# Splitting a tile's softmax probabilities one tile later, with exp written to PSUM

## The chip, the cores and the metric

The kernel runs on one core of a Trainium2 chip. The metric is device time in microseconds (us) for one execution, from the median of several runs. Engines are named as the profile names them: PE is TensorE's matmul, PEld its weight load, DVE is VectorE, ACT is ScalarE, POOL is GpSimd, and SP is SyncE, which issues every DMA of this kernel. Each engine works through its own instructions strictly in order and waits for the others by semaphores.

## The reference, cut to what matters

The reference is a two-layer decoder trunk on 1024 tokens of width 1024, in float32. Layer 0 is a pooling branch plus an attention into 256 memory tokens. Layer 1, where the change lies, has a "forgetting" attention with 16 heads of width 64. For each block of 128 queries it computes this:

```python
logits = jnp.einsum('bqhd,bkhd->bhqk', qi, k, preferred_element_type=jnp.float32) * scale
logits = logits + (ci[..., :, None] - cum_k[:, :, None, :])
qpos = s0 + jnp.arange(Q_BLOCK)
mask = kpos[None, :] <= qpos[:, None]
logits = jnp.where(mask[None, None], logits, -jnp.inf)
p = jax.nn.softmax(logits, axis=-1)
return jnp.einsum('bhqk,bkhd->bqhd', p.astype(v.dtype), v)
```

The mask is causal, so query block i needs only the first (i + 1) * 128 keys. The attention's output is gated, goes with the memory branch through an output projection, and ends in a residual LayerNorm.

## The kernel before, in words

The forgetting attention is the function `fox`. It goes over 16 heads (`hd`), and in each over 8 tiles of 128 queries (`i`), 128 steps in all. Two heads make a pair (`pr`, `b`). Tile i has L = (i + 1) * 128 keys, so it grows from 128x128 to 128x1024. A PSUM bank holds 512 columns, so tiles 4 to 7 are made in two parts (384 + 256, 512 + 256, 512 + 384, 512 + 512).

One step of the softmax, `probs` (L637), is a chain over four engines. The kernel works with negated logits and so with a minimum.

- POOL writes the forget-gate term and the causal mask into a tile `p` of the pool "P" (L643, L644).
- PE makes the logits into a PSUM bank of the tag "L", which has two banks (L649).
- DVE adds the two, keeps the result in `p` and takes the running minimum of the row (L650). This releases the "L" bank.
- ACT computes exp in place in `p` and sums the rows (L652), then writes the high float16 half of the scaled probabilities into a second tile, `two` (L654).
- DVE makes the low half of them, the scaled probability minus its high half (L655). Here and below this is the subtract.

Then `turn` (L672) has SP issue a DMA transpose of `two` (L676), and three steps later `values` (L678) multiplies the turned probabilities of two tiles with the values on PE (into PSUM tag "O", one bank). `inverses` (L658) takes the reciprocal of the row sums of a pair, has PE turn it into PSUM tag "T" (L662), and brings it through DRAM into a tile R, broadcast (L664, L667). `pair_out` (L698) multiplies the pair's output with it (L700), gates it (L702) and stores it (L703).

Two things set the order of the work. PE's order is written out by hand (`manual_schedule`): in each step the logits, then 40% of the step's share of filling matmuls, then the transpose and the values, then 60% of the fill. The fill (`Fill`) is the projection work of the next pair and of the gates, in `slab` (L184, PSUM tag "pj", three banks), whose results ACT and DVE evacuate (L197, L198, L591, L592, L601, L602, L613). The other engines' orders are chosen by a planner from the dependencies; that also picks which of the four buffers of the pool "P" a tile gets. `p` and `two` share those four. The list `past` holds the last three tiles (LAG), so that `values` and `inverses` come the right number of steps later.

The weights of the final output projection are loaded into buffers that the attention leaves free, in the order of `wtags` (L762).

Of the kernel before, what the change touches and what calls it, by code (L numbers as in the profile page):

```python
# [9 lines left out]
F32 = mybir.dt.float32  # L10
# [4 lines left out]
AF = mybir.ActivationFunctionType  # L15
ALU = mybir.AluOpType
AX = mybir.AxisListType

P = 128
# [3 lines left out]
ST = S // P  # L23
NH = 512
HEADS = 16
# [10 lines left out]
LAG = 3  # L36
APART = 6 * NH
PSCALE = 2.0 ** 15
# [33 lines left out]
def trunk_kernel(ctx, tc, x, xT, memT, win, wk, wv0, wv, wmk, wmv, wout, poolw, pscale, lng, lnb, bforget, out):  # L72
# [35 lines left out]

    def T(shape=(P, S), dt=F32R):
        return sb(list(shape), "T", 6, dt)  # L110
# [10 lines left out]
    def tiny(n, dt=F32):  # L121
        return small.tile([P, n], dt, tag=f"s{n}{dt}", name=nm("s"))
# [37 lines left out]
        nc.vector.memset(invc[:, t : t + 1], 1.0 / (t + 1))  # L160
    psc = const.tile([P, 8], F32, name="psc")
    pschalf = const.tile([P, 8], F32, name="pschalf")
    edge = const.tile([P, 48], F32, name="edge")
    nc.vector.memset(edge, 0.0)
    inverse = const.tile([P, P], F32, name="inverse")
    nc.vector.memset(inverse, 0.0)
# [241 lines left out]
    with tc.tile_pool(name="in0", bufs=1) as in0:  # L408
# [56 lines left out]
        wtags = [("MK", 4)] * 2 + [("W", 4)] * 2 + [("B", 8)] * 4 + [("Y", 4)] * 2 + [("PG", 0), ("w", 0)]  # L465
# [4 lines left out]
    with tc.tile_pool(name="in1", bufs=1) as in1:  # L470
# [163 lines left out]
            nc.sync.dma_start(R, cumd[hd].partition_broadcast(P))  # L634
            return R

        def probs(hd, i, R, sums):  # L637

            q, kx, ky = pairs[hd // 2][hd % 2]
            L = (i + 1) * P  # L640
            qs = slice(i * P, L)
            p = sb([P, S], "P", 4)
            nc.gpsimd.tensor_scalar(p[:, :L], R[:, :L], 1.0, cumn[:, i * HEADS + hd : i * HEADS + hd + 1], ALU.mult, ALU.add)  # L643
            nc.gpsimd.affine_select(p[:, qs], p[:, qs], [[-1, P]], ALU.is_ge, -NEG, base=0, channel_multiplier=1)  # L644
            m = tiny(2)
            top = -NEG
            for n, (lo, up) in enumerate([(0, L)] if L <= NH else [(0, 384), (384, L)] if L == 640 else [(0, NH), (NH, L)]):
                lg = ps([P, NH], "L", 2)[:, : up - lo]
                mm3(lg, ((q[:, qs], kx[:, lo:up]), (q[:, qs], ky[:, lo:up])))  # L649
                nc.vector.tensor_tensor_reduce(p[:, lo:up], lg, p[:, lo:up], 1.0, top, ALU.add, ALU.min, m[:, n : n + 1])  # L650
                top = m[:, n : n + 1]
            nc.scalar.activation(p[:, :L], p[:, :L], AF.Exp, bias=top, scale=-1.0, accum_out=sums[:, 8 * (hd % 2) + i : 8 * (hd % 2) + i + 1])  # L652
            two = sb([P, 2 * S], "P", 4, F16)
            nc.scalar.activation(two[:, :L], p[:, :L], AF.Copy, scale=PSCALE)  # L654
            nc.vector.scalar_tensor_tensor(two[:, L : 2 * L], p[:, :L], PSCALE, two[:, :L], ALU.mult, ALU.subtract)  # L655
            return two

        def inverses(pr, sums):  # L658

            nc.vector.reciprocal(inverse[:, : 2 * ST], sums)  # L660
            t = ps([P, 4, P], "T", 2)
            nc.tensor.transpose(t[:, 0, :], inverse, ident)  # L662
# [9 lines left out]
        def turn(hd, i, two):  # L672

            n = 2 * i + 2
            pt[hd, i] = T([P, 2 * ST, P], F16)
            nc.sync.dma_start_transpose(pt[hd, i][:, :n, :], two[:, : n * P])  # L676
# [32 lines left out]
            pair_out(pr, o, None, g)  # L709

        def fox(following):
            fill, past = Fill(), [None] * LAG
            gs, ws = {}, {}

            def gate_ahead(pr):
                gs[pr] = G()
                fill.add(gate_units(win[1, 12 + pr], gs[pr], XH, XL), SLAB)

            for hd in range(HEADS + 1):
                pr, b = divmod(hd, 2)  # L720
                if hd < HEADS:
                    if b == 0:
                        o, sums = G(), tiny(2 * ST)
                        if 0 < pr < 7:
                            fill.add(pair_units(pr + 1), 3 * SLAB)
                        for ahead in {0: (0, 1), 2: (2,), 4: (4,), 7: (7,)}.get(pr, ()):
                            gate_ahead(ahead)
                        if pr == 0:
                            fill.add(following, SLAB)
                        for late in (3, 5, 6) if pr == 7 else ():  # L730
                            fill.add(late_gate(late), SLAB)
                    R = forget_rows(hd)
                for i in range(ST if hd < HEADS else LAG):
                    ahead = sum(SHARE[i:]) + (sum(SHARE) if b == 0 else 0) + (sum(SHARE[:LAG]) if pr == 7 else 0)
                    part = fill.left * SHARE[i] / (ahead if hd < HEADS else sum(SHARE[i:LAG]))
                    new = None
# [88 lines left out]
```

## Time and profile before

| | us |
|---|---|
| median of 3 runs | 1413.47 (1410.78 to 1415.64) |
| the profiled execution | 1409.78 |
| its span, first to last instruction | 1408.1 |
| PE busy | 1303.5 |
| DVE busy | 773.1 |
| ACT busy | 532.1 |
| POOL busy | 287.0 |

The profile is of one execution. Of its span, the first 0 to about 700 us are layer 0 and the start of layer 1, about 700 to 1252 us are the 128 steps of `fox`, and from about 1268 us on the output projection runs. A row of the waits names the waiting engine and tile, what ended the wait, the sum, the number and the longest. A row of the timeline gives the start and the duration in us, the engine, the line, the operation, and in brackets the idle time just before it and what ended that. A matmul's busy time reaches past the moment at which the next one may start, so PE is idle somewhat more than one minus its busy share.

### The profile page before, as it was taken

To read this page: it belongs to the slowest core of one execution; us is meant where nothing else is said; L and a number is where in the kernel's file an instruction comes from. 1 tells how busy PE (TensorE), PEld (TensorE's weight loads), DVE (VectorE), ACT (ScalarE), POOL (GpSimd) and SP (SyncE) were. 2 spreads that over 40 slices of the span, in tenths; PEclk is the share of its full clock that TensorE was granted. 3 is DMA by queue.
4 is the path that set the end of the run, shared out by engine and by line. 5 is a ranking of instruction groups with operands and counts; after the bars stand their busy time and mean duration, and the time that the engine had idled before them with its cause. 6 is when DMAs were issued, how large, how long until landed. Compare 5 with 4: busy or idle time off the path is not lost. (4 is left out here: it accounts for less than half of the span.)

```text
span 1408.1 us, 19081 instructions
## 1 busy us (share of the span) xinstructions
PE 1303.5 (93%) x6866; PEld 1057.4 (75%) x6866; DVE 773.1 (55%) x1566; ACT 532.1 (38%) x1052; POOL 287.0 (20%) x380
## 2 busy tenths in 40 slices
PE   9999999999999999999988788888898888869997
PEld 6878888887788878889766566756776656658886
DVE  6434665546555553664555655556556565565553
ACT  5333432214311242542354544454545554452110
POOL 0000000000000000000254545445454444530000
PEclk9999999999999999999999999999999999889999
DMA  5431122124633351114465768676767686685331
GB/s 202 135 102 41 31 97 60 68 78 160 225 113 108 102 150 51 32 29 139 92 144 109 166 138 173 118 159 155 156 128 157 133 168 140 171 227 170 124 127 48
DMA packets 234063, 173.44 MB, mean 123 GB/s; under 512 B 175728, under 2 KB 189296, under 8 KB 233968
## 3 DMA queue, kind: packets, MB, share of 16 engines
q1 hardware_dynamic: 233968, 172.22, 47.0%
q8 instruction: 54, 0.88, 0.3%
q14 instruction: 41, 0.34, 0.1%
HBM read 99.17 MB, written 22.68 MB: 87 GB/s over the span
## 5 line engine op out<-in xcount | busy, mean ns | idle before, releaser
L184 PE MATMUL pj<-A,w 128*128 128x512 f32 x2928 | 736.6, 399 | 1.5 <-DVE MK L143 1.1
L184 PEld LDWEIGHTS pj<-A,w 128*128 128x128 f32 x2928 | 544.4, 191 | 106.7 <-DVE MK L143 2.0
L655 DVE SCALAR_TENSOR_TENSOR P<-P,P 128x128 f16<-128x128 f32 (+7 forms) x128 | 108.5, 850 | 137.4 <-ACT P L654 137.3
L652 ACT ACTIVATE P<-P,s 128x128 f32<-128x128 f32 (+7 forms) x128 | 99.2, 775 | 183.4 <-DVE s L650 183.2
L172 PE MATMUL L<-B,B 128*128 128x512 f32 (+3 forms) x384 | 106.6, 370 | 60.0 <-DVE s L650 59.1
L172 PEld LDWEIGHTS L<-B,B 128*128 128x128 f32 x384 | 66.4, 193 | 105.5 <-DVE s L650 84.3
L153 DVE TENSOR_TENSOR w<-raw,w 128x512 fp32r<-128x512 f32 x102 | 70.0, 689 | 119.1 <-ACT w L152 118.3
L643 POOL TENSOR_SCALAR P<-R,cumn 128x128 f32<-128x128 f32 (+7 forms) x128 | 101.0, 789 | 159.4 <-DVE P L655 139.7
L564 POOL MEMSET G<- 128x128 f32 x1 | 0.2, 204 | 636.4 <-DVE V L318 636.4
L152 ACT CAST w<-raw 128x512 fp32r<-128x512 f32 x102 | 63.2, 622 | 159.4 <-PE pj L184 104.0
L654 ACT ACTIVATE P<-P 128x128 f16<-128x128 f32 (+7 forms) x128 | 87.4, 683 | 21.2 <-DMA T<-P 18.2
L650 DVE CUSTOM_DVE_ANT_0 P<-L,P 128x512 f32<-128x512 f32 (+3 forms) x128 | 73.0, 570 | 40.4 <-POOL P L644 26.7
L142 ACT CAST T<-T 128x512 fp32r<-128x512 f32 (+1 forms) x56 | 42.6, 788 | 137.2 <-DMA T<-y1d 55.4
L172 PEld LDWEIGHTS <-V 128*128 128x128 f16 x1152 | 72.4, 104 | 25.3 <-issue 23.6
L172 PE MATMUL O<-T,V 128*128 128x128 f16 x1152 | 83.5, 230 | 8.0 <-DMA T<-P 8.0
L143 DVE TENSOR_TENSOR T<-T,T 128x512 fp32r<-128x512 f32 (+1 forms) x56 | 50.0, 916 | 74.2 <-PE L L349 63.6
L153 POOL TENSOR_TENSOR w<-raw,w 128x512 fp32r<-128x512 f32 x54 | 77.2, 1429 | 4.1 <-PE pj L184 1.0
L150 POOL TENSOR_SCALAR w<-raw 128x512 fp32r<-128x512 f32 x54 | 40.7, 754 | 143.6 <-PE pj L184 143.6
L349 PE MATMUL pj<-B,T 128*128 128x512 f32 x216 | 52.3, 390 | 0.6 <-DVE B L143 0.6
L349 PE MATMUL L<-B,T 128*128 128x512 f32 x216 | 51.9, 389 | 0.0
L644 POOL TENSOR_SCALAR_AFFINE_SELECT P<-P 128x128 f32<-128x128 f32 x128 | 48.5, 379 | 8.2
L349 PEld LDWEIGHTS pj<-B,T 128*128 128x128 f32 x216 | 40.7, 189 | 9.5 <-DVE B L143 1.0
(183 smaller groups left out, 1571.3 us busy)
## 6 DMA issues: line engine op xcount, KB each, us to landing
raw<-in_win_dram SPq DMA_DIRECT2D x96, 256.0 KB, 2.7
raw<-in_wout_dram SPq DMA_DIRECT2D x48, 256.0 KB, 3.7
B<-B SPq DMA_DIRECT2D x64, 128.0 KB, 2.4
R<-cumd SPq DMA_DIRECT2D x16, 512.0 KB, 4.3
y0d<-Y SPq DMA_DIRECT2D x12, 512.0 KB, 3.0
T<-y0d SPq DMA_DIRECT2D x12, 512.0 KB, 4.1
T<-y1d SPq DMA_DIRECT2D x12, 512.0 KB, 4.3
raw<-in_wmk_dram SPq DMA_DIRECT2D x16, 256.0 KB, 2.7
```

The costliest lines, as they stand in the source:

```text
L143: nc.vector.tensor_tensor(lo, src, hi.bitcast(F32), ALU.subtract)
L152: nc.scalar.copy(h, r)
L153: (nc.gpsimd if low[0] else nc.vector).tensor_tensor(l, r, h.bitcast(F32), ALU.subtract)
L172: nc.tensor.matmul(acc, a, b, start=i == 0, stop=i == len(terms) - 1)
L184: nc.tensor.matmul(accs[n], a[:, k, :], b[:, kt, n * NH : (n + 1) * NH], start=kt == 0 and i == 0, stop=kt == KT - 1 and i == 2,)
L349: nc.tensor.matmul(accs[a][nh], y[:, k, a * P : (a + 1) * P], w, start=kt == 8 and i == 0, stop=kt == 7 and i == 2,)
L643: nc.gpsimd.tensor_scalar(p[:, :L], R[:, :L], 1.0, cumn[:, i * HEADS + hd : i * HEADS + hd + 1], ALU.mult, ALU.add)
L644: nc.gpsimd.affine_select(p[:, qs], p[:, qs], [[-1, P]], ALU.is_ge, -NEG, base=0, channel_multiplier=1)
L650: nc.vector.tensor_tensor_reduce(p[:, lo:up], lg, p[:, lo:up], 1.0, top, ALU.add, ALU.min, m[:, n : n + 1])
L652: nc.scalar.activation(p[:, :L], p[:, :L], AF.Exp, bias=top, scale=-1.0, accum_out=sums[:, 8 * (hd % 2) + i : 8 * (hd % 2) + i + 1])
L654: nc.scalar.activation(two[:, :L], p[:, :L], AF.Copy, scale=PSCALE)
L655: nc.vector.scalar_tensor_tensor(two[:, L : 2 * L], p[:, :L], PSCALE, two[:, :L], ALU.mult, ALU.subtract)
```

## The change

`probs` no longer makes the two float16 halves. It ends with exp, which now writes into one or two PSUM banks of the tag "T" (two banks, until now used for a few transposes) instead of back into `p`, a separate instruction with its own row sum for each part of the tile. The halves are made by a new function `halves`, which is called (by `behind`) in the next tile's `probs`, between that tile's minimum and its exp. It reads the probabilities from PSUM, and works part by part. The transposes and the sums' reciprocals follow one step later; `values` stays where it was, three steps behind the logits. The row sums now have two columns per tile, the second one zeroed by a memset for tiles of one part, and are added before the reciprocal.

Beside this, paddings change: the constant `edge` is 40 instead of 48 wide, and with the new small tiles every large tile starts at a multiple of 256 bytes within its partition; before, every large tile started 32 bytes past such a multiple. And in the order of the weight buffers, one pair of "V" buffers moves from the ninth place to the third.

```diff
-    edge = const.tile([P, 48], F32, name="edge")
+    edge = const.tile([P, 40], F32, name="edge")
...
-        def probs(hd, i, R, sums):
+        def probs(hd, i, R, sums, behind):
...
-            nc.scalar.activation(p[:, :L], p[:, :L], AF.Exp, bias=top, scale=-1.0, accum_out=sums[:, 8 * (hd % 2) + i : 8 * (hd % 2) + i + 1])
+            behind()
+            es = []
+            for n, (lo, up) in enumerate(parts):
+                e = ps([P, NH], "T", 2)[:, : up - lo]
+                nc.scalar.activation(
+                    e, p[:, lo:up], AF.Exp, bias=top, scale=-1.0, accum_out=sums[:, n, hd % 2, i : i + 1],
+                )
+                es.append((lo, up, e))
+            return hd, i, es
+
+        def halves(hd, i, es):
+
+            L = (i + 1) * P
             two = sb([P, 2 * S], "P", 4, F16)
-            nc.scalar.activation(two[:, :L], p[:, :L], AF.Copy, scale=PSCALE)
-            nc.vector.scalar_tensor_tensor(two[:, L : 2 * L], p[:, :L], PSCALE, two[:, :L], ALU.mult, ALU.subtract)
-            return two
+            for lo, up, e in es:
+                nc.scalar.activation(two[:, lo:up], e, AF.Copy, scale=PSCALE)
+                nc.vector.scalar_tensor_tensor(two[:, L + lo : L + up], e, PSCALE, two[:, lo:up], ALU.mult, ALU.subtract)
+            return hd, i, two
...
-            nc.vector.reciprocal(inverse[:, : 2 * ST], sums)
+            both = sb([P, 64], "both", 1, F32, small)[:, : 2 * ST]
+            nc.vector.tensor_tensor(
+                both.rearrange("p (b i) -> p b i", b=2), sums[:, 0], sums[:, 1], ALU.add,
+            )
+            nc.vector.reciprocal(inverse[:, : 2 * ST], both)
...
-                        o, sums = G(), tiny(2 * ST)
+                        o, sums = G(), sb([P, 4 * ST], "sums", 2, F32, small).rearrange("p (n b i) -> p n b i", n=2, b=2)
+                        nc.vector.memset(sums[:, 1], 0.0)
...
-                    new = None
+                    new, split = None, []
+
+                    def behind():
+                        if fresh[0]:
+                            split.append(halves(*fresh[0]))
+                            fresh[0] = None
+
                     if hd < HEADS:
                         new = (hd, i, o, sums)
-                        two = probs(hd, i, R, sums)
+                        fresh[0] = probs(hd, i, R, sums, behind)
+                    else:
+                        behind()
                     fill.pump(part * FRAC[0])
-                    if new:
-                        turn(hd, i, two)
-                    old, older = past[-1], past[0]
+                    for what in split:
+                        turn(*what)
+                    old, older = past[-2 if hd < HEADS else -1], past[0]
...
-        wtags = [("MK", 4)] * 2 + [("B", 10)] * 5 + [("R", 2), ("V", 4), ("V", 4), ("PG", 0), ("w", 0)]
+        wtags = [("MK", 4)] * 2 + [("V", 4)] + [("B", 10)] * 5 + [("R", 2), ("V", 4), ("PG", 0), ("w", 0)]
```

More of the change, by code (lines that the diff above doesn't have):

```diff
@@ L646, in probs @@
             top = -NEG
-            for n, (lo, up) in enumerate([(0, L)] if L <= NH else [(0, 384), (384, L)] if L == 640 else [(0, NH), (NH, L)]):
+            parts = [(0, L)] if L <= NH else [(0, 384), (384, L)] if L == 640 else [(0, NH), (NH, L)]
+            for n, (lo, up) in enumerate(parts):
                 lg = ps([P, NH], "L", 2)[:, : up - lo]
@@ L651, in probs @@
                 top = m[:, n : n + 1]
-            nc.scalar.activation(p[:, :L], p[:, :L], AF.Exp, bias=top, scale=-1.0, accum_out=sums[:, 8 * (hd % 2) + i : 8 * (hd % 2) + i + 1])
+            behind()
+            es = []
+            for n, (lo, up) in enumerate(parts):
+                e = ps([P, NH], "T", 2)[:, : up - lo]
[6 more added lines that the diff above has]
+            L = (i + 1) * P
             two = sb([P, 2 * S], "P", 4, F16)
-            nc.scalar.activation(two[:, :L], p[:, :L], AF.Copy, scale=PSCALE)
-            nc.vector.scalar_tensor_tensor(two[:, L : 2 * L], p[:, :L], PSCALE, two[:, :L], ALU.mult, ALU.subtract)
-            return two
+            for lo, up, e in es:
+                nc.scalar.activation(two[:, lo:up], e, AF.Copy, scale=PSCALE)
+                nc.vector.scalar_tensor_tensor(two[:, L + lo : L + up], e, PSCALE, two[:, lo:up], ALU.mult, ALU.subtract)
+            return hd, i, two
         def inverses(pr, sums):
-            nc.vector.reciprocal(inverse[:, : 2 * ST], sums)
+            both = sb([P, 64], "both", 1, F32, small)[:, : 2 * ST]
[3 more added lines that the diff above has]
+            nc.vector.reciprocal(inverse[:, : 2 * ST], both)
             t = ps([P, 4, P], "T", 2)
@@ L711, in fox @@
         def fox(following):
-            fill, past = Fill(), [None] * LAG
+            fill, past, fresh = Fill(), [None] * LAG, [None]
             gs, ws = {}, {}
```

## The prediction

> **What bounds the kernel now.** I read the page first, then the windows for the stretch of `fox`, then the waits, then the timeline of a few steps, then the groups by shape.
>
> ```profile
> span 1408.1 us, 19081 instructions
> 700.00:1252.00 552.00, 472.33 (x2775) 364.04 (x2774) 323.33 (x713) 278.05 (x554) 274.82 (x365) 0.96 0.69 151
> 1274.20 5.44 PE L L349 x24
> L184 PE MATMUL pj<-A,w 128*128 128x512 f32 x1269 | 339.1, 406 | 0.0
> ```
>
> The second row is the window of `fox`: length, then busy time of PE, PEld, DVE, ACT, POOL, then the granted clock and the DMA share. PE is busy 472 of 552 us, DVE 323, ACT 278, so PE is the bound and loses 80 us there. The third row, from the chain that ended last, prices dense work: 24 matmuls of 512 columns in 5.44 us, 0.227 us each. The fourth row says that PE never waited for the fill: what it waits for is named here (engine and tile, releaser: us, times, longest):
>
> ```profile
> PE L L172 <- DVE s L650: 59.1, 57, 2.8
> PE T L662 <- DVE inverse L660: 11.5, 7, 4.3
> PE O L172 <- DMA T<-P: 8.0, 7, 2.5
> DVE P L655 <- ACT P L654: 137.3, 109, 2.3
> POOL P L643 <- DVE P L655: 139.7, 46, 5.2
> ACT P L652 <- DVE s L650: 183.2, 108, 5.2
> ```
>
> The first three add up to 78.6 of the 80 us. The largest is PE waiting for an "L" bank, which DVE's minimum (L650) releases. One step shows why that comes late:
>
> ```profile
> 928.92 0.60 DVE L650 CUSTOM_DVE_ANT_0 P<-L,P,s 128x384 f32<-128x384 f32 x1
> 929.56 1.04 ACT L652 ACTIVATE P<-P,s 128x896 f32<-128x896 f32 x1 [2.56 <-DVE s L650]
> 930.73 0.95 ACT L654 ACTIVATE P<-P 128x896 f16<-128x896 f32 x1
> 931.71 1.09 DVE L655 SCALAR_TENSOR_TENSOR P<-P,P 128x896 f16<-128x896 f32 x1 [2.19 <-ACT P L654]
> 932.72 0.68 DVE L650 CUSTOM_DVE_ANT_0 P<-L,P 128x512 f32<-128x512 f32 x1
> 933.47 0.44 PE L172 MATMUL L<-B,B 128*128 128x128 f32 x2 [1.10 <-DVE s L650]
> ```
>
> DVE finishes tile 6's minimum at 929.52, then sits 2.19 us in front of the subtract (L655) until ACT has done exp and the high half. The next minimum stands behind the subtract, starts at 932.72, and PE waits 1.10 us for it. So in the large tiles the time is set by a ring: minimum, exp, high half, subtract, next minimum. The 137.3 us above are this idle time of DVE.
>
> **The change, part by part.**
>
> *The subtract goes behind the next minimum.* In the changed program's order DVE has, for nearly all of the two-part tiles, both minima of tile i before the two subtracts of tile i-1 (in the smallest tiles some subtracts still come first). The minimum then waits only for logits and mask. The mask's buffer comes free after exp instead of after the subtract, which takes the ground from most of POOL's 139.7 us, and the planner's choice of buffers changes: before, in 15 places, a tile's `p` takes the buffer of the `p` just before it; after, never. Does DVE keep up once the ring is open? Its prices:
>
> ```profile
> L650 DVE CUSTOM_DVE_ANT_0 P<-L,P 128x512 f32<-128x512 f32 x64 | 43.9, 687 | 6.1 <-PE L L172 2.8 <-POOL P L644 1.1 <-POOL P L643 1.0
> L650 DVE CUSTOM_DVE_ANT_0 P<-L,P,s 128x512 f32<-128x512 f32 x16 | 12.0, 751 | 1.8 <-DVE s L650 1.6
> L650 DVE DVE_READ_ACCUMULATOR2_ANT s<- 128x1 f32 x192 | 15.7, 82 | 0.0
> L602 DVE SCALAR_TENSOR_TENSOR B<-pj,B 64x512 fp32r<-64x512 f32 x28 | 19.3, 689 | 7.8 <-ACT B L601 7.1
> L655 DVE SCALAR_TENSOR_TENSOR P<-P,P 128x1024 f16<-128x1024 f32 x16 | 19.6, 1225 | 12.6 <-ACT P L654 12.6
> L693 DVE TENSOR_TENSOR G<-O,G 64x256 f32<-64x256 f32 x62 | 25.9, 418 | 3.2 <-ACT G L692 2.3
> ```
>
> Step 7, the largest: two minima 0.69 + 0.75 and their two reads 0.16; two subtracts from PSUM, of which no row exists: the nearest is L602, the same operation on 512 columns with one operand in PSUM, 0.689 us, so 1.38 at most; evacuations of fill and output, some 0.6 us a step (L602 and L693 with their likes, about 73 us over 128 steps). Together 3.6 us. Steps 6 and 5 come by their widths to about 3.2 and 2.9, so 9.7 for three steps. PE in the same three: 9.9 fill matmuls a step (1269 over 128) at 0.227, 6.7; logits of 4, 3.5 and 3 widths of 512, 2.4; half a pair of values, 0.9; 10.0 us. So the two are level, with DVE no longer behind; in the other steps PE has more to do. Level engines still show their hand-offs. I allow two of 0.2 us in each of these three steps, about 1.3 us per head, 21 us in 16 heads. Of the 59.1 us, then, 38 go. Ends: none of it goes if the ring closes elsewhere (rival D), all 59 if the hand-offs overlap.
>
> *DVE's longer subtracts and small extras.* Two of 0.689 against one of 1.225 is +0.15 us for 64 tiles, at most 10 us on an engine that is idle 229 of 552 us; I take nothing, since the idle time in front of L655 covers it, and it is in the 3.6 us above. The add and memset per pair are 16 columns wide each and ride in the same gaps; uncovered they would be 16 times about 0.25 us, 4 us.
>
> *ACT: two exps and two copies in place of one.*
>
> ```profile
> L652 ACT ACTIVATE P<-P,s 128x512 f32<-128x512 f32 x16 | 11.6, 724 | 29.5 <-DVE s L650 29.5
> L652 ACT ACTIVATE P<-P,s 128x1024 f32<-128x1024 f32 x16 | 18.4, 1149 | 18.1 <-DVE s L650 18.1
> L652 ACT ACTIVATION_READ_ACCUMULATOR P<-P,s 128x1 f32 x128 | 23.9, 186 | 0.0
> L654 ACT ACTIVATE P<-P 128x1024 f16<-128x1024 f32 x16 | 16.9, 1057 | 0.5
> L613 ACT COPY MK<-pj 128x512 f32<-128x512 f32 x12 | 7.0, 580 | 3.1 <-PE pj L184 3.0
> ```
>
> Exp 2 x 0.724 - 1.149 = 0.30, one more row-sum read 0.19, copies 2 x 0.580 (from PSUM, L613) - 1.057 = 0.10: 0.59 us for 64 tiles, 38 us. ACT goes from 278 to 316 of 552 us. An exp that writes PSUM has no row; at L613's 0.580, the nearest with PSUM on one side, it would save 0.14 each, at L652's 0.724 nothing. I take 0.724, the same function. None of this lies on PE's path as long as ACT's step (two exps with reads 1.82, two copies 1.16, fill and output copies about 0.6: 3.6 us in step 7) is hidden behind PE; against PE's 3.1 us there it is 0.5 us over, but in step 0 after it ACT has less than 2 us of work.
>
> [...]
>
> *The "T" banks make a new ring.* Exp of tile i, part a, needs the bank that the subtract of tile i-1, part a, still reads. Ring: exp a 0.91 with its read, exp b 0.91, copy a 0.58, subtract a 0.69, and four hand-offs of about 0.15: 3.7 us per step, against 552/128 = 4.3 us that a step takes now. It fits, so I take nothing; from above it is rival D. What stands behind a waiting exp on ACT are the fill's evacuations and the output copies; PE has three "pj" banks and shows no wait for them now (the 0.0 above).
>
> *The reciprocal moves a step later.* PE reaches the transpose L662 one step after the last exp instead of in the same step:
>
> ```profile
> 1250.03 0.47 PE L662 MATMUL T<-ident,inverse 128*128 128x128 f32 x1 [4.33 <-DVE inverse L660]
> 912.69 1.28 DVE L700 SCALAR_TENSOR_TENSOR G<-G,unscale,R 128x1024 f32<-128x1024 f32 x1 [2.54 <-DMA R<-invd]
> DVE G L700 <- DMA R<-invd: 6.2, 3, 2.5
> ```
>
> The waits in front of it go, except the last, 4.33 us at the end, where the order stays as it was: 11.5 - 4.3 = 7 us. The path through DRAM then has one step less before L700, whose wait blocks DVE's later minima. But the fourth tile's minimum stands now ahead of L700, and the write of the rows no longer stands behind the wait for exp. I take the same 6 us as now; at most, with the longest wait at all 8 pairs, 20 us of DVE, some 10 on PE.
>
> *The DMA transposes move.* Each is issued after a subtract that now stands behind a minimum, while `values` stays three steps behind the logits.
>
> ```profile
> 943.20 1.05 PE L172 MATMUL O<-T,V 128*128 128x128 f16 x16 [1.46 <-DMA T<-P]
> T<-P SPq DMA_TRANSPOSE x128, 3.7
> POOL w L150 <- PE pj L184: 88.4, 39, 4.9
> ```
>
> After tile 7's minimum come exp (two with reads, 1.8), copy a and b (1.2) and the last subtract 0.7, with the wait for the bank about 0.9 us later than now. In 7 of 16 heads PE already waits there, so 7 x 0.9 = 6 us more. Ends: 8 us less, if the earlier minima hand the time back, and 24 more (rival C). On SP the weight loads stand behind the later transposes; the row of L150 covers it, POOL waits there for PE's free buffers and not for data, 2.3 us at a time. If that cover went, it would show as PE waits on L184.
>
> *256-byte alignment.* No row tells the two apart. The nearest is the 3.7 us from issue to landing of a transpose. Bounds: nothing, and the whole 8.0 us of PE's wait for them. I take nothing.
>
> ```profile
> DMA packets 234063, 173.44 MB, mean 123 GB/s; under 512 B 175728, under 2 KB 189296, under 8 KB 233968
> ```
>
> [...]
>
> *One pair of "V" buffers earlier at the end.*
>
> ```profile
> 1266.34 1.22 PE L349 MATMUL pj<-MK,T 128*128 128x512 f32 x2 [5.59 <-ACT T L142]
> ```
>
> PE's wait before the output projection is for data (T), not for weights, so nothing; bounds 0 and -5.6.
>
> **Sum.** On the profiled execution: span 1408.1 and 1.7 around it, 1409.8; -38 (L) -7 (reciprocal) +6 (transposes) = -39, so 1370.8. The median of the runs is 3.7 us above the profiled one; carried over, 1374 us.
>
> **The rivals.**
>
> A, the forecast: the ring opens, some hand-offs stay; 1374, by the ends of its terms 1355 to 1395. For it: DVE's 137.3 us of idle lie exactly where the minimum wants to go.
>
> B, nearly everything goes: all of L and the reciprocal, 66 us, the transposes no later: 1413 - 66 = 1347. For it: PE has more work than DVE in five of eight steps. Against it: they are level in the other three.
>
> C, the wait moves to the values: a subtract that is a step later costs PE 2 us per head on "O" (the longest now is 2.5) instead of 0.5: 24 in place of 6, so 1374 + 18 = 1392, and with the other half of L's gain lost as well up to 1405. For it: seven such waits already. Against it: the minima before it come earlier, too.
>
> D, slower: the "T" ring becomes the bound. If each exp waits for the subtract and that stands behind both minima, the ring is minima 1.6 + subtract a 0.69 + exps 1.82 + copy a 0.58 + hand-offs 0.6 = 5.3 us. Now the minima of tiles 6 and 7 start at 927.97 and 932.72, 4.75 us apart. 0.55 us more for three tiles in 16 heads is +26, less the 7 of the reciprocal: 1433. It decides where both minima can't start before the bank's subtract is due, that is if logits or masks come late. Against it: PE's logits for the next tile are only one "L" bank away.
>
> ```profile
> 927.97 0.69 DVE L650 CUSTOM_DVE_ANT_0 P<-L,P 128x512 f32<-128x512 f32 x1
> ```
>
> E, no change: what PE gains in `fox` is lost in the same steps to ACT's 38 us; 1413.
>
> **How the numbers follow.** A 0.47, B 0.14, C 0.15, D 0.18, E 0.06. About 0.3%, 4 us, is what a measurement of this kernel can tell from no change. Faster is A, B and C, 0.76; same 0.06; slower 0.18. The range runs from below B, with a few us for alignment and tail, 1340, to 1412, which leaves out D and the far end of B. For A alone it is 1355 to 1395.
>
> **What would show each step.** Right: PE's wait for L650 falls below 25 us in `fox`, DVE's wait for the copy from 137 us to below 60, in the timeline minima directly behind the logits and ahead of the subtract, and PE's wait for the reciprocal only at the end. Wrong by C: "PE O" waits for "T<-P" above 20 us. Wrong by D: ACT's exp waits for DVE's subtract, and PE's wait for L650 stays near 59 us. Wrong by alignment: transposes landing well below 3.7 us.

## The result

The changed kernel takes 1345.05 us in the median (1342.89 to 1347.01, 4 runs). The kernel before, on the same chip, takes 1412.80 (1410.78 to 1415.64, 4 runs). The ratio is 0.9519, with a 95% interval of 0.9495 to 0.9542: 68 us faster, where 39 were forecast.

### The profile page after: what moved, and what is told of

Read it like the earlier page. It is cut to its first block, busy times and chain, and to the rows that moved or that the text cites. A ratio compares the mean times of both kernels' runs of the same rounds, so it can differ in the third digit from the quotient of the medians.

```text
span 1344.4 us, 19414 instructions
## 1 busy us (share of the span) xinstructions
PE 1276.5 (95%) x6866; PEld 1056.7 (79%) x6866; DVE 766.2 (57%) x1646; ACT 549.0 (41%) x1244; POOL 264.5 (20%) x380
## 4 chain that ended last, share of the span: by engine, by line
PE 71%; DMA 13%; DVE 7%; ACT 4%; issue 2%; POOL 1%; SPq 1%; DVEq 0%; ACTq 0%; POOLq 0%
PE pj L184 38%; PE pj L349 9%; PE L L349 8%; DMA T<-P 8%; PE L L172 5%; PE O L172 5%; DMA raw<-in_wout_dram 2%; PE pj L537 2%; PE T L239 1%; PE pj L172 1%; DMA raw<-in_wmv_dram 1%; ACT T L659 1%; PE pj L215 1%; DVE w L153 1%; PE L L184 1%
## 5 line engine op out<-in xcount | busy, mean ns | idle before, releaser
L659 ACT ACTIVATE T<-P,s 128x128 f32<-128x128 f32 (+2 forms) x192 | 111.1, 578 | 108.4 <-DVE s L653 82.9
L153 DVE TENSOR_TENSOR w<-raw,w 128x512 fp32r<-128x512 f32 x102 | 70.0, 689 | 118.5 <-ACT w L152 115.7
L671 DVE SCALAR_TENSOR_TENSOR P<-T,P 128x128 f16<-128x128 f32 (+2 forms) x192 | 102.6, 553 | 55.8 <-ACT P L670 55.0
L653 DVE CUSTOM_DVE_ANT_0 P<-L,P 128x512 f32<-128x512 f32 (+3 forms) x128 | 73.1, 571 | 54.9 <-PE L L172 35.7
L172 PE MATMUL L<-B,B 128*128 128x512 f32 (+3 forms) x384 | 92.0, 346 | 6.3 <-DVE s L653 6.2
L172 PE MATMUL O<-T,V 128*128 128x128 f16 x1152 | 79.6, 222 | 18.3 <-DMA T<-P 18.3
L172 PEld LDWEIGHTS <-V 128*128 128x128 f16 x1152 | 66.7, 99 | 38.5 <-issue 37.5
L670 ACT ACTIVATE P<-T 128x128 f16<-128x128 f32 (+2 forms) x192 | 86.8, 484 | 16.2 <-DMA T<-P 14.1
L172 PEld LDWEIGHTS L<-B,B 128*128 128x128 f32 x384 | 71.9, 191 | 25.1 <-DVE s L653 11.1
L153 POOL TENSOR_TENSOR w<-raw,w 128x512 fp32r<-128x512 f32 x54 | 69.5, 1287 | 3.3
L150 POOL TENSOR_SCALAR w<-raw 128x512 fp32r<-128x512 f32 x54 | 35.8, 663 | 95.3 <-PE pj L184 95.2
L349 PEld LDWEIGHTS L<-B,T 128*128 128x128 f32 x216 | 40.5, 188 | 8.4
```

The source lines that it names most:

```text
L153: (nc.gpsimd if low[0] else nc.vector).tensor_tensor(l, r, h.bitcast(F32), ALU.subtract)
L172: nc.tensor.matmul(acc, a, b, start=i == 0, stop=i == len(terms) - 1)
L349: nc.tensor.matmul(accs[a][nh], y[:, k, a * P : (a + 1) * P], w, start=kt == 8 and i == 0, stop=kt == 7 and i == 2,)
L659: nc.scalar.activation(e, p[:, lo:up], AF.Exp, bias=top, scale=-1.0, accum_out=sums[:, n, hd % 2, i : i + 1],)
L670: nc.scalar.activation(two[:, lo:up], e, AF.Copy, scale=PSCALE)
L671: nc.vector.scalar_tensor_tensor(two[:, L + lo : L + up], e, PSCALE, two[:, lo:up], ALU.mult, ALU.subtract)
```

## The profile after

The windows of the kernel before: length, busy time of PE, PEld, DVE, ACT and POOL, then the granted clock, the DMA share and GB/s. The stretches are `fox` and the gap between it and the output projection, which goes from there to the end of the span.

```profile
699.30:1260.80 561.50, 481.78 (x2841) 371.77 (x2839) 325.66 (x718) 279.88 (x558) 275.44 (x366) 0.96 0.70 152
1260.80:1268.00 7.20, 1.27 (x3) 0.56 (x3) 4.79 (x4) 3.48 (x5) 4.65 (x2) 0.67 0.70 268
```

The same view of the changed kernel, the stretches cut at the same events:

```profile
698.30:1191.40 493.10, 453.36 (x2840) 368.91 (x2839) 312.80 (x789) 294.39 (x744) 252.30 (x366) 0.98 0.75 170
1191.40:1203.00 11.60, 1.40 (x3) 0.68 (x4) 9.85 (x8) 4.45 (x7) 5.11 (x2) 0.63 0.68 224
```

The whole gain is in `fox`: 561.5 to 493.1 us, or 68.4. It starts 1.0 us earlier; behind it the gap loses 4.4 us, and the projection 1.3 (141.4 us to the end of the span at 1344.4, against 140.1 to 1408.1). Within `fox` the 68.4 us have two halves. PE's idle time falls from 79.7 (561.50 - 481.78) to 39.7 us, by 40.0. And PE's busy time falls by 28.4 us for the same matmuls.

The waits of the changed kernel (us, times, longest), those that answer to the rows shown of before:

```profile
DVE P L671 <- ACT P L670: 55.0, 58, 2.4
POOL P L645 <- DMA T<-P: 52.9, 22, 5.0
ACT T L659 <- DVE P L671: 20.6, 20, 1.8
PE O L172 <- DMA T<-P: 18.3, 17, 2.8
PE T L682 <- DVE P L671: 12.8, 7, 3.1
PE L L172 <- DVE s L653: 6.2, 8, 1.9
PE T L682 <- DVE inverse L680: 2.3, 1, 2.3
```

PE's wait for the minimum (L650 before, L653 now) went from 59.1 to 6.2 us. DVE's wait for the copy went from 137.3 to 55.0. Two waits did not do as forecast. PE still stands in front of the transpose of the reciprocals (L662 before, L682 now), 15.1 us in place of 11.5, now mostly for a subtract. And it stands 18.3 us for the turned probabilities, 8.0 before.

The timeline of the changed kernel in two large tiles shows the new order (start, duration, engine, line; idle time before it in brackets):

```profile
926.63 0.69 DVE L653 CUSTOM_DVE_ANT_0 P<-L,P 128x512 f32<-128x512 f32 x1 [0.84 <-PE L L172]
927.50 0.62 DVE L653 CUSTOM_DVE_ANT_0 P<-L,P,s 128x384 f32<-128x384 f32 x1 [0.17 <-DVE s L653]
928.04 1.02 DVE L671 SCALAR_TENSOR_TENSOR P<-T,P 128x512 f16<-128x512 f32 x2
928.82 0.69 ACT L659 ACTIVATE T<-P,s 128x512 f32<-128x512 f32 x1 [1.25 <-DVE P L671]
```

Both minima of a tile run ahead of the previous tile's two subtracts, and DVE waits for PE's logits (0.84 us in the first row), no longer PE for DVE. The fourth row is the ring of the "T" banks: exp waits for the subtract to free its bank. ACT stands 20.6 us there in all.

## The experiments

**Only the order, without PSUM.** The halves come a tile later as in the change, but exp stays in SBUF, in place and in one piece; padding and weight order are those of the changed kernel.

```diff
-            for n, (lo, up) in enumerate(parts):
-                e = ps([P, NH], "T", 2)[:, : up - lo]
+            for n, (lo, up) in enumerate([(0, L)]):
+                e = p[:, :L]
```

> The changed kernel, but exp stays in SBUF, in place in p, in one piece with one copy and one subtract per tile; only the step behind which the halves are made is as in the changed kernel (and its padding and weight order). Theory O (the order opens the ring): most of the gain of 68 us is here, 1345 to 1370. Rival S (the subtract's operand in PSUM frees DVE from POOL and the P buffers): less than a third of the gain, above 1390.

Measured: 1366.8 us (1361.41 to 1370.59), ratio 0.9691 (0.9658 to 0.9724). Its waits:

```profile
POOL P L645 <- DMA T<-P: 125.9, 61, 4.7
PE O L172 <- DMA T<-P: 30.9, 22, 3.1
PE pj L349 <- ACT T L142: 17.0, 1, 17.0
PE L L172 <- DVE s L653: 13.5, 17, 1.7
PE T L682 <- DVE inverse L680: 5.0, 1, 5.0
```

PE's wait for the minimum is down to 13.5 us here too, against 54.5 in the padded kernel before (below), so it is the order that opens the ring. PE's wait for the reciprocals is down to the last pair, which is what the prediction had said; the T banks are free here. Two things keep this kernel behind the changed one. In `fox` it is the "P" buffers: `p` is kept until the late subtract has read it, POOL waits 125.9 us (52.9 in the changed kernel) for a transpose to give a buffer back, and the transposes come late for the values. Behind `fox` it is the 17.0 us that PE waits for the first operand of the output projection, 7.0 in the changed kernel. The edit has also changed the order in which SP issues its DMAs: the load of that operand (`T<-y1d`) is issued 11.5 us after the end of the last values, and 3.6 us in the changed kernel.

**Only PSUM, without the order.** exp by parts into "T" banks, the halves made in the same step as before; padding and weight order of the changed kernel.

```diff
-            behind()
             es = []
...
                         fresh[0] = probs(hd, i, R, sums, behind)
-                    else:
                         behind()
...
-                    old, older = past[-2 if hd < HEADS else -1], past[0]
+                    old, older = past[-1], past[0]
```

> The changed kernel with exp in PSUM by parts, but the halves made in the same step as exp, transposes and reciprocals in the steps of before. Theory O: the ring of minimum, exp, copy, subtract, next minimum is closed again, 1395 to 1420, PE's wait for the minimum 40 to 60 us. Rival S: 1345 to 1370, PE's wait for the minimum below 25 us.

Measured: 1401.76 us (1397.29 to 1402.91), ratio 0.9936 (0.9913 to 0.9959). Its waits:

```profile
DVE P L670 <- ACT P L669: 126.1, 102, 2.4
PE L L172 <- DVE s L653: 36.8, 40, 1.9
PE T L681 <- DVE sums L743: 19.1, 6, 3.6
PE T L681 <- DVE P L670: 8.8, 2, 6.1
```

DVE still stands in front of the subtract for exp and copy, 126.1 us, so the ring stays. It costs PE less, though: 36.8 us, under the 40 to 60 that were expected and 18 less than the 54.5 of the padded kernel before (below). What PE gains there it loses in front of the reciprocals' transpose, 27.9 us (19.1 + 8.8) in place of 12.1. The releasers named are the memset of the second sums, which came with the change, and a subtract, which reads a "T" bank. So the small difference from the padded kernel before, 1 us, is a gain and a loss together.

**Only the padding, taken back.** One constant of the changed kernel is 48 wide again. Every large tile then starts 32 bytes past a multiple of 256; the instructions and their order on each engine are the same but for that memset's width.

```diff
-    edge = const.tile([P, 40], F32, name="edge")
+    edge = const.tile([P, 48], F32, name="edge")
```

> The changed kernel with every large tile 32 bytes past a multiple of 256 again. If alignment does nothing: 1345 within 4 us, transposes 3.6 us from issue to landing. If the alignment carries a part of the gain: 1355 or more, transposes slower and PE's wait for them above the 18.3 us of the changed kernel.

Measured: 1366.18 us (1361.5 to 1368.24), ratio 0.9685 (0.9660 to 0.9709). By the ratios the padding is worth 0.0166 of 1411, 23 us, in the changed kernel; by the medians of the two chips 21. PE's waits, and then the DMA issues (the last number is the median time from issue to landing):

```profile
PE O L172 <- DMA T<-P: 23.9, 16, 2.9
PE T L682 <- DVE P L671: 14.3, 7, 3.6
PE L L172 <- DVE s L653: 10.6, 10, 2.2
PE T L682 <- DVE inverse L680: 2.9, 1, 2.9
```

```profile
T<-P SPq DMA_TRANSPOSE x128, 4.0
V<-MK SPq DMA_TRANSPOSE x16, 4.5
```

The DMA issues of the changed kernel:

```profile
T<-P SPq DMA_TRANSPOSE x128, 3.6
V<-MK SPq DMA_TRANSPOSE x16, 3.5
```

Between the two profiled executions `fox` differs by 19.2 us (the table of stretches below). PE's four waits make 12.1 of them, and each of the four is longer; PE's busy time, 459.0 in place of 453.4 us, makes most of the rest.

**Only the padding, in the kernel before.** The same constant, the other way round.

```diff
-    edge = const.tile([P, 48], F32, name="edge")
+    edge = const.tile([P, 40], F32, name="edge")
```

> The kernel before with every large tile at a multiple of 256 bytes and nothing else changed. If alignment does nothing: 1413 within 4 us. If it carries a part: below 1405, with transposes landing sooner than the 3.7 us of before.

Measured: 1402.57 us (1392.02 to 1407.27, 7 runs), ratio 0.9929 (0.9905 to 0.9953): 8 to 10 us. PE's waits:

```profile
PE L L172 <- DVE s L650: 54.5, 51, 3.4
PE O L172 <- DMA T<-P: 1.8, 3, 0.8
```

The profile is of the slowest of the seven runs (1407.27). Transposes land after 3.3 us in place of 3.7, and the wait at the values falls from 8.0 to 1.8; that upper bound of the prediction, 8.0, was about right for this kernel. The ring of the minimum keeps the rest.

These four and the two kernels give a table of the three parts (us, medians; the corner that is the changed kernel is from another chip):

| | exp in SBUF | exp in PSUM |
|---|---|---|
| halves in the same step, padded to 256 | 1402.6 | 1401.8 |
| halves a tile later, padded to 256 | 1366.8 | 1345.1 |
| halves in the same step, not padded | 1410.8 | not run |
| halves a tile later, not padded | not run | 1366.2 |

The order is worth 36 us with exp in SBUF and 57 in PSUM. PSUM is worth 1 us without the order and 22 with it. The padding is worth 8 at the start and 21 at the end. The parts don't add up one by one. A reading that fits the waits, but that no run tests by itself, is that each of the last two shortens a path (the P buffers, the turned probabilities) on which PE stands longer once the ring is open. The corners of PSUM hold more than that: without the order its gain at the minimum is lost at the reciprocals' transpose, and with it the profiled executions differ by 12.6 us in `fox` and by 10.0 in the gap behind it, with 7.2 the other way ahead of `fox` and in the projection.

The profiled executions by stretch (us, from their timelines) show it. The stretches are the time up to the first logits of `fox`, from there to the end of the last values, the gap up to the first matmul of the output projection, and the rest of the span:

| | ahead of `fox` | `fox` | gap | projection |
|---|---|---|---|---|
| kernel before | 699.3 | 560.0 | 7.0 | 141.7 |
| only the padding | 703.0 | 553.6 | 7.6 | 141.3 |
| only PSUM | 696.5 | 553.1 | 8.5 | 143.1 |
| only the order | 694.4 | 504.3 | 18.4 | 142.6 |
| changed, padding back | 693.8 | 510.9 | 10.1 | 145.0 |
| changed kernel | 698.1 | 491.7 | 8.5 | 146.1 |

In `fox` alone the order is worth 49 us with exp in SBUF and 61 in PSUM, PSUM 0.5 without the order and 12.6 with it, the padding 6.4 at the start and 19.2 at the end. The stretch ahead of `fox`, where the kernels do the same work but for their padding, varies by 9 us, so a few us between two spans say little by themselves.

**Where the padding acts.** Three kernels shift one group of buffers each by 32 bytes and leave the rest at multiples of 256; all engines' orders are those of the changed kernel. The sources of the transposes first (a tile of 32 bytes ahead of the pool "P", one of 224 behind it, room taken from the small tiles):

```diff
+        first = tag == "P" and not around
+        if first:
+            around.append(1)
+            nc.vector.memset(sb([P, 8], "px", 1), 0.0)
+        t = (where or pool).tile(shape, dt, tag=tag, name=nm(tag), bufs=bufs)
+        if first:
+            nc.vector.memset(sb([P, 56], "py", 1), 0.0)
+        return t
```

> The changed kernel with only the four buffers P (the f32 logits and the f16 halves, the source of the probabilities' transposes) 32 bytes past a multiple of 256; their destination, the operands of PE, the values and everything else large stay at multiples of 256. Putting back the padding shifted all of them and cost 21 us (1366). Theory: the sources of the transposes carry it, so most of the 21 us is here: 1358 to 1366, with the transposes of the probabilities landing in 3.9 to 4.1 us in place of 3.6 and those of V unchanged at 3.5. Rival: it is the destinations, or operands and results of the engines elsewhere: then 1345 to 1350 with 3.6 us.

Measured: 1353.98 us (1351.01 to 1360.57), ratio 0.9608 (0.9578 to 0.9637). Its DMA issues:

```profile
T<-P SPq DMA_TRANSPOSE x128, 3.9
V<-MK SPq DMA_TRANSPOSE x16, 3.5
```

The probabilities' transposes land 0.3 us later than in the changed kernel; those of V, whose source stayed in place, do not. The time is 4 us short of what the theory wanted: the sources carry 9 to 13 us, about half. In `fox` the profiled execution is 12.1 us longer than the changed kernel (503.8 against 491.7), of the 19.2 for the whole padding. The P buffers also hold what the engines work on, but the busy time of DVE, ACT and POOL stays (767.2, 549.8 and 263.0 us against 766.2, 549.0 and 264.5), so it is the transposes that pay. The same with the pool "T", where the transposes land (`tag == "T"` in the first line):

> The changed kernel (1345 us) with only the six buffers T (where the DMA transposes of the probabilities land, and TensorE's operands there) 32 bytes past a multiple of 256. Theory: the sources cost 9 us (1354 with the P buffers alone off) and the whole shift 21 us, so another 12 us lie elsewhere; if they lie in the destination of the transposes, this gives 1352 to 1358, with the transposes landing in 3.8 to 4.0 us. Rival: the destination's place costs nothing (1343 to 1348, 3.6 us), and the rest is in the other buffers (K, Q, V, gates, broadcast rows).

Measured: 1350.24 us (1347.36 to 1352.59), ratio 0.9587 (0.9561 to 0.9614), 3.7 us to landing. That is under the expected range and above the rival's, and the landing is short of the 3.8 to 4.0 us expected. On this chip the changed kernel with only the weight order put back (below) took 1344.55 (1342.38 to 1346.56), so the offset of the T buffers costs about 6 us. But the transposes land after 3.7 us there too, and `fox` is no longer here than there, 490.2 us against 491.0. What the two profiled executions differ by lies in the projection (149.2 against 144.7) and ahead of `fox` (699.1 against 695.7), where the T buffers take other loads. So the runs do not show that the destination of the probabilities' transposes costs anything. And with the buffers B, V and R, by one more pad of 32 bytes among the small tiles:

```diff
-    for _ in range(4):
-        nc.vector.memset(small.tile([P, 8], F32, tag="edge", name="edge"), 0.0)
+    for _ in range(1):
+        nc.vector.memset(small.tile([P, 40], F32, tag="edge", name="edge", bufs=1), 0.0)
```

> The changed kernel with only the buffers B, V and R (keys, queries, the transposed V halves, the broadcast rows and gate factors) and small ones 32 bytes past a multiple of 256. If the rest of the 21 us is in what VectorE and TensorE read there, or in where the transposes of V land: 1350 to 1358, and V's transposes at 4.0 to 4.5 us in place of 3.5. If the transposes' source and destination are all: 1343 to 1348.

Measured: 1348.74 us (1342.49 to 1353.85), ratio 0.9576 (0.9537 to 0.9614), transposes at 3.6 and 3.5 us. Its runs overlap those of 1344.55, so this group's 4 us are not settled, and `fox` is not longer (490.3 us). In `fox`, then, the sources of the transposes carry 12 of the 19 us and the other two groups alone nothing. The other 7 show only when all are shifted together, and stay open; that the three costs add up to 19 to 23 us is no proof, since they lie in different stretches.

What an offset at the source does to the transposes is measured: 3.9 us to landing in place of 3.6. The mechanism behind it is not shown, since the rows give the time to landing and not what happens within a transfer.

**The weight order of the output projection**, put back in the changed kernel:

```diff
-        wtags = [("MK", 4)] * 2 + [("V", 4)] + [("B", 10)] * 5 + [("R", 2), ("V", 4), ("PG", 0), ("w", 0)]
+        wtags = [("MK", 4)] * 2 + [("B", 10)] * 5 + [("R", 2), ("V", 4), ("V", 4), ("PG", 0), ("w", 0)]
```

> The changed kernel with the slots of the last projection's weights as before (V fifth of the B group's successors, not third). The stretch between the last values and the projection went from 7.2 to 11.6 us with the change, and PE's longest waits there are for the split of the last transposed tile (7.0 us for ACT, 3.3 us for DVE), not for weights. Theory: the order of the weights is worth nothing by itself: 1343 to 1348. Rivals: the V slots, free later than the B ones, hold the projection up now (time 1339 to 1342 with the old order), or the old order would (1348 to 1352).

Measured: 1344.55 us (1342.38 to 1346.56), ratio 0.9547 (0.9522 to 0.9573). It is worth nothing. PE's wait there is still for the split of the last turned tile (8.6 us for ACT and 2.7 for DVE here, 7.0 and 3.6 in the changed kernel), so the 4.4 us lost in the gap are not due to the order of the weights. The timeline of the changed kernel shows where they lie:

```profile
1193.44 0.58 SPq L341 DMA_DIRECT2D T<-y1d  x1
```

This is the load of the projection's first operand. It is issued 3.6 us after the end of the last values (1189.86), behind three weight loads that SP issues first; in the kernel before it was issued 1.9 us ahead of that end. PE's second wait there, 3.3 us, is for the low half of the same operand, which DVE makes behind those of three weights.

**The wait that took the reciprocals' place.** The transpose of the reciprocals gets a slab bank in place of a "T" bank.

```diff
-            t = ps([P, 4, P], "T", 2)
+            t = ps([P, 4, P], "pj", 3)
             nc.tensor.transpose(t[:, 0, :], inverse, ident)
```

> The changed kernel (1345 us) with one edit: the PSUM tile of the reciprocal's transpose comes from the three slab banks (pj) in place of the two banks T that the exps now hold. Theory: in the changed kernel PE stands 12.8 us (7 waits) at this transpose for a bank T that a subtract still reads, and 2.3 us for the reciprocal. If the bank is what it waits for, both shrink to the 4 us of the last pair and the time falls to 1332 to 1338. Rival: PE only reaches the next wait sooner (the transposed probabilities, 18.3 us in 17 waits), and the time stays within 3 us of 1345; a third way is that the slabs now stand for their own bank, and the time goes above 1348.

Measured: 1341.49 us (1329.68 to 1341.71), ratio 0.9492 (0.9452 to 0.9533), no difference from the changed kernel that these runs can tell. It is above the theory's range. Three of the four runs lie within 0.4 us of each other, and why the fourth took 1329.68 is open. Its waits:

```profile
PE O L172 <- DMA T<-P: 25.2, 22, 3.1
PE L L172 <- DVE s L653: 9.8, 11, 2.7
PE pj L682 <- DVE inverse L680: 3.9, 1, 3.9
PE pj L682 <- DVE B L602: 1.0, 2, 0.8
```

So it was the bank: of 15.1 us at this transpose 4.9 remain. But PE then stands 6.9 us more at the values and 3.6 more at the logits, 10.5 together, as much as the 10.2 that went, which is the rival's mechanism.

**One step more for the transposes.**

```diff
-LAG = 3
+LAG = 4
```

> The changed kernel with LAG 4 in place of 3: the values of a tile, and the reciprocal, come one step later. Theory: PE's 18.3 us of waits (17) at the values are the probabilities' DMA transposes, which the change issues a step later at an unchanged LAG; with another step between them nearly all of it goes and the time falls to 1328 to 1336. Rival: what is late is the softmax chain itself (POOL, DVE and ACT taking turns), PE then stands for the minimum at the logits in place of the values (6.2 us now, 15 to 25 then), and the time stays within 4 us of 1345.

Measured: 1334.26 us (1332.84 to 1337.06), ratio 0.9464 (0.9447 to 0.9481), in the range of the theory. Its waits:

```profile
PE T L682 <- DVE P L671: 12.8, 5, 4.6
PE L L172 <- DVE s L653: 12.5, 15, 2.2
PE T L682 <- DVE inverse L680: 5.9, 1, 5.9
PE T L682 <- DVE sums L744: 3.1, 2, 1.6
PE O L172 <- DMA T<-P: 0.2, 1, 0.2
```

The 18.3 us at the values are gone. At the logits 6.3 of them come back, and at the reciprocals' transpose 6.7 (21.8 against 15.1). So `fox` gains little, 2.5 us (489.2 in place of 491.7). Of the 13.3 us between the two profiled executions 5.2 lie in the gap and 4.9 in the projection: the load of its first operand is now issued 2.3 us ahead of the end of the last values, and PE's two waits there are 1.8 and 1.6 us in place of 7.0 and 3.6. The theory was right about the wait at the values, but the time came into its range by luck, from stretches that it had not counted.

**Both.**

> Both edits, the reciprocal's transpose on a slab bank and LAG 4. Theory: the two waits are separate (12.8 + 2.3 us and 18.3 us), so the gains add: 1316 to 1326. Rival: either edit alone moves the wait to the chain of the softmax, and both together give no more than the better of the two alone (1330 to 1345).

Measured: 1328.34 us (1327.89 to 1331.02), ratio 0.9424 (0.9406 to 0.9443). It falls between the two theories. By the medians it is 16.7 us below the changed kernel, where the two edits alone gave 3.6 and 10.8, and less than the waits that they were to remove. In `fox` both give 7.6 us (484.1), and each alone 0.9 and 2.5: there either edit alone moves most of its wait to the place that the other one relieves. Its waits:

```profile
PE L L172 <- DVE s L653: 13.8, 16, 2.3
PE pj L682 <- DVE B L602: 10.5, 5, 4.1
PE pj L682 <- DVE inverse L680: 5.9, 1, 5.9
```

The transpose now stands for a slab bank that a fill's evacuation (L602) still reads. This version does all of the work and is faster than both kernels, 1.0% (by the ratios) to 1.2% (by the medians) below the changed one. With the old weight order on top:

> The kernel with the reciprocal's transpose on a slab bank and LAG 4 (1328.3 us), and the old order of the last weights. With the order worth nothing: 1326 to 1331. With V's slots freed a step later by LAG 4, the changed order (V third) could now wait for them, and the old one be faster by 2 to 5 us: 1323 to 1326.

Measured: 1329.34 us (1328.46 to 1332.7), ratio 0.9446 (0.9417 to 0.9476), the same.

## Why the prediction was right, and where it was off

The direction, the ring and its opening were right, and the time lies in the range. The forecast of 1374 is 29 us too high. With the padding taken back the changed kernel takes 1366, 8 us from the forecast, which had counted the padding as nothing. So about 21 of the 29 us are that term. That the rest is so near is partly luck: with the padding back PE's idle time in `fox` falls by 28 us (79.7 to 51.9), where 39 were forecast, and its busy time by 21 (480.3 to 459.0), which no term had.

- *The ring.* "The 137.3 us above are this idle time of DVE": shown by the order alone, which cuts PE's wait for the minimum from 54.5 to 13.5 us with exp still in SBUF. The term was -38 of 59.1; measured -53, to 6.2 us. What was too large is the allowance for hand-offs, 0.2 us twice in three large steps per head. No row gave that figure (and 2 x 3 x 0.2 is 1.2 us per head, 19 in all, not 1.3 and 21). The timeline shows why they cost less: in the step shown DVE waits for the logits. This is rival B's size for this term.
- *What the term was measured in.* The sum was made of PE's idle time alone. By coincidence that sum came out: idle fell by 40.0, and -39 was forecast, the larger gain at the ring having been eaten by the two misses below. The 28.4 us of PE's busy time were in no term. One group by shape, before and then after:

```profile
L172 PE MATMUL L<-B,B 128*128 128x512 f32 x160 | 55.2, 428 | 20.5 <-DVE s L650 19.5
```

```profile
L172 PE MATMUL L<-B,B 128*128 128x512 f32 x160 | 47.4, 393 | 2.0 <-DVE s L653 1.9
```

The same 160 logits matmuls take 428 ns each before and 393 after. PE's busy time over the whole span goes with the order alone: 1303.5, 1304.3 (PSUM only) and 1306.0 (padding only) with the halves in the same step, and 1274.3 (order only), 1279.6 (padding back) and 1276.5 with the halves a tile later. The granted clock in `fox` rises from 0.96 to 0.98; by an estimate from these two figures, 482 us x (1 - 0.96 / 0.98), that could be about 10 of the 28. But the changed kernel with the padding back has 0.96 in `fox`, as the kernel before (0.980 and 0.978 over the whole span), and 21 us less busy time; and with PSUM only the clock is 0.93 (0.966 over the span) and the busy time 483.1. So the clock is not the main part. Another part may be the end of the matmul ahead of each wait, with which nothing overlaps. An estimate from the rows in the prediction: a fill matmul is busy for 0.406 us and a dense one takes 0.227, so 0.18 us for each wait; PE's main waits in the rows above go from 71 to 33, which is about 7 us. The rest stays open.
- *"The waits in front of it go, except the last, 4.33 us."* Wrong: 15.1 us in place of 4.3. The reciprocal does come in time, but its transpose then waits for a "T" bank, one of the two that the exps now hold. The timeline of the changed kernel:

```profile
936.35 0.25 DVE L680 RECIPROCAL inverse<-both 128x16 f32<-128x16 f32 x1
939.61 0.29 DVE L671 SCALAR_TENSOR_TENSOR P<-T,P 128x128 f16<-128x128 f32 x1
939.95 0.33 PE L682 MATMUL T<-ident,inverse 128*128 128x128 f32 x1 [1.53 <-DVE P L671]
```

  The reciprocal is ready at 936.60, and the transpose starts at 939.95, behind a subtract. The prediction had taken the ring of the "T" banks for exp alone and forgot their old user. With exp in SBUF the wait is 5.0 us, with another bank 4.9.
- *The transposes.* +6 was forecast at the values and +10.3 measured; 20 us, rival C's sign, was not reached. LAG 4 shows that it is the step which the halves lost.
- *256-byte alignment.* "I take nothing", with 8.0 us as the other end. Wrong by 21 us in the changed kernel, and by more than the bound. No row stood behind the nothing, and the bound was read off PE's wait in the kernel before, where the padding measures 8. In the changed kernel all four of PE's waits grow when the padding comes back, the one at the values by 5.6 us and the other three by 6.5, so a bound from the one wait of the kernel before was too narrow. The mark set for this, transposes landing well below 3.7 us, was a bad one: between two programs with different DMA traffic (152 and 170 GB/s in `fox`) it showed 3.6, and within one program 4.0 against 3.6.
- *The ends.* V's weight order at nothing was right. The 4.7 us lost outside `fox` were in no term.
- *exp into PSUM, ACT's 38 us, DVE's longer subtracts.* None showed on PE's path, as forecast, but for the bank in front of the reciprocals' transpose. Two sizes were off: ACT's busy time in `fox` rose by 14.5 us (279.9 to 294.4) and not 38, and DVE's subtracts did not cost up to 10 us more: their busy time fell from 108.5 to 102.6 us. The rows of the changed kernel:

```profile
L659 ACT ACTIVATE T<-P,s 128x512 f32<-128x512 f32 x80 | 55.0, 688 | 63.6 <-DVE s L653 38.4 <-DVE P L671 20.6 <-POOL w L153 2.2
L671 DVE SCALAR_TENSOR_TENSOR P<-T,P 128x512 f16<-128x512 f32 x80 | 53.6, 687 | 23.7 <-ACT P L670 23.1
```

  An exp of 512 columns takes 688 ns into PSUM and 724 into SBUF, which was the value taken, with 580 as the other end. The subtract with one operand in PSUM is 687, as taken from L602.
- *The rivals.* D's ring is there (ACT waits 20.6 us for the subtract) but it doesn't decide: PE's wait for the minimum, which was to stay near 59 us, is 6.2. A's mechanism is nearest to what happened; the time is B's, by way of the padding and PE's busy time.

## What to carry to other kernels

What the stalls of the bounding engine cost here was not its idle time alone: 40 us less idle came with 28 us less busy time for the same matmuls. A cost that is hidden now, or bounded by a small wait now, has to be priced again in the kernel after the change, on the path that will be bare then; the padding was worth 8 us before and 21 after. A time that comes out as expected is no proof of the mechanism until one has seen in which stretch it was won: with LAG 4 it was not the attention. And when a resource gets a new, frequent user (the two "T" banks), look for its old users.

## What the runs showed of the hardware beside that

32 bytes of offset on all large buffers cost 21 us in the changed kernel, 1.6% of it, and 8 us in the kernel before, with the instructions unchanged but for the width of one memset. Of the 19 us in `fox`, 12 come with the source buffers of the DMA transposes alone, which then land after 3.9 us in place of 3.6.

And POOL took less time for the same 380 instructions: its 54 operations of L153 on weights went from 1429 to 1287 ns each, its 128 masks (L644 before, L646 now) from 379 to 332. POOL's busy time over the span is 287.0 us in the kernel before, 288.9 with only the padding and 288.1 with only the order, where the subtract reads both operands from SBUF. It is 266.4 us with only PSUM, 265.2 with the padding back and 264.5 in the changed kernel, where it reads one from PSUM. So it goes with exp in PSUM and not with the order. DVE's side, in the kernel before and then with only the order:

```profile
L655 DVE SCALAR_TENSOR_TENSOR P<-P,P 128x512 f16<-128x512 f32 x16 | 12.9, 804 | 17.1 <-ACT P L654 17.0
L153 DVE TENSOR_TENSOR w<-raw,w 128x512 fp32r<-128x512 f32 x102 | 70.0, 689 | 119.1 <-ACT w L152 118.3 <-PE pj L215 0.6
```

```profile
L671 DVE SCALAR_TENSOR_TENSOR P<-P,P 128x512 f16<-128x512 f32 x16 | 13.8, 864 | 6.0 <-ACT P L670 5.9
```

A subtract of 512 columns with both operands in SBUF takes 804 to 864 ns beside POOL's work, and 687 with one of them in PSUM. The second row is another subtract of DVE with both operands in SBUF, on weights; all of its 102 run before POOL begins its own work on weights (the last starts at 679.8 us, POOL's first at 683.0), and it takes 689. That speaks against the place of the operands alone, and for that place together with POOL's work, though the two rows are not the same operation. How the two engines would hold each other up, no row shows.
